# First stage of a two-block transformer kernel: a new written order, and the B matrices turned whole

## The chip, the cores and the metric

The kernel runs on one core of one Trainium2 chip. The metric is the device time of one execution in microseconds (us). A change within about 0.2% of it can't be told from no change.

## The reference, cut to what matters

Two transformer blocks stand one after the other, on 256 tokens of 1024 features, all float32. Only the beginning of both matters here.

The first block modulates its input: for the latent stream `x` and the context stream `ctx`

```
mod_lat = silu(c) @ ada_w[0] + ada_b[0]
sh1, sc1, ga1, sh2, sc2, ga2 = split(mod_lat, 6)
u_lat = rms_norm(x, g_mix[0]) * (1 + sc1) + sh1
qkv   = u_lat @ na_wqkv
```

and the same with `c_ctx` and `ctx`. So the first large product, `@ na_wqkv`, needs the first two sixths (shift and scale) of `c @ ada_w`, which is 8 MB of weights.

The second block has a state-space mixer (S5) with 64 groups of 64 complex states. Its recurrence is computed in chunks of 8 tokens by operator matrices which depend on the weights `lam`, `log_dt`, `B`, `C`, `d` alone. They are wanted only late in the kernel, but they are built at its very start.

## The kernel before, in words

Every large product is split in three float32r products (high by high, high by low, low by high part); `Weights` (from line 245) loads a weight tile (`raw`), writes its high part `whi` by ScalarE (ACT) and its low part `wlo` by VectorE (DVE), in `split`, whose operations have the lines 109 and 112 of the helpers `act` and `tt`.

The **first stage** is the code from line 942 to `spp.close()`. In it

- small vectors, constants, `x`, `ctx` and the S5 weights are loaded. `s5_load` (line 574) loads B (`a_b_re`, `a_b_im`) in two halves each, with the 32 pairs of groups on 32 partitions, into tiles `bt`, and C into tiles `ci`;
- `S5.__init__` (line 600) turns B: for each of the 16 features `h_` there is a turn of 32x64 numbers for the first group of each pair (`T.transpose`, line 620) and, for the second group, a product with the 32x32 identity that writes the lower 64 rows of the result (`T.matmul`, line 618). DVE then makes `bb` and the powers `pw`;
- `x` and `ctx` are turned by TensorE (PE, line 982) and copied to `h` and `hc` by ACT;
- `ada_steps(0, 0)` and `ada_steps(0, 1)` (line 347) are 16 steps, 8 for shift and 8 for scale. A step loads 512 KB of `ada_w` and multiplies; even steps load into a pool of three tiles `ada`, odd steps into two tiles `stl` that later hold the normed input. The eighth step of each row of steps ends in `adacc` (DVE), two turns (PE, line 367) and `mods` (DVE); the last also gives `scg`. `ada(n)` is the next n steps;
- `rstd` (line 442) squares `h` and `hc` on ACT, sums on PE (line 428), takes the reciprocal on DVE (line 432) and spreads it by PE (line 439); `prep_vectors` (line 211) turns the small vectors (line 214) into `vt`;
- `s5.c()` (line 703) turns C and makes `dd`; `s5.e(r)` (line 733) makes the matrices `e` of operator group r on DVE: 8 products into `tm` and 4 sums into `e`, all 128x512. `operators(r)` (line 968) is `k1` (PE, from `e` and `cbk`), `et` (four turns of `e` on PE, four copies on ACT, four stores to `edr`) and `k2`. There are four groups, r = 0 to 3;
- `normed` (line 461) makes the normed, modulated input `x` in high and low parts: for each of 8 feature tiles and both streams `t` (DVE), `xh` (ACT), `xl` (DVE).

The second stage then begins with the product for the first head pair (`lead`, 96 matmuls of 128x256) and for the first group of values (another 96), lines 302 to 304; its other tiles lie in pools opened after the tiles `e`, `kt` and their like are given back (`spp.close()`).

**What sets the order.** Each engine runs its instructions in one compiled order. Inside `tc.manual_schedule(...)` (line 974) the engines named, and that is all of them, take the instructions in the order in which they are written. Behind the block a scheduler orders the instructions by its own model, before the run; it may also put such later instructions between those of the block. A DMA is issued by the queue of the engine on which it is written: SP (`dma`), ACT (`dma_a`) or POOL (`G.dma_start`). The four `raw` loads of `w_first` are written on SP between steps 10 and 11 of the modulation.

Of the kernel before, what the change touches and what calls it, by code (L numbers as in the profile page):

```python
# [8 lines left out]
F32 = mybir.dt.float32  # L9
# [73 lines left out]
def _build(ctx, tc, I, out, dbg):  # L83
    nc = tc.nc
    V, A, G, T = nc.vector, nc.scalar, nc.gpsimd, nc.tensor
    MUL, ADD, SUB = ALU.mult, ALU.add, ALU.subtract
    dma, dma_a = nc.sync.dma_start, nc.scalar.dma_start
# [26 lines left out]
    def stt(o, a, s, b, op0, op1):  # L114
        V.scalar_tensor_tensor(out=o, in0=a, scalar=s, in1=b, op0=op0, op1=op1)  # L115

    def ts(o, a, s1, op0, s2=None, op1=None, e=None):
        e = e or V
        if s2 is None:
            e.tensor_scalar(out=o, in0=a, scalar1=s1, scalar2=None, op0=op0)  # L120
        else:
            e.tensor_scalar(out=o, in0=a, scalar1=s1, scalar2=s2, op0=op0, op1=op1)
# [18 lines left out]
    cst = const.tile([128, _NC], F32, name="cst")  # L141
# [25 lines left out]
    gsw = [swg[:, 0:64], swg[:, 64:128]]  # L167
# [221 lines left out]
    def modcol(l, n, kt, v):  # L389
        return mods[l][:, n * 8 + kt, v:v + 1]  # L390
# [92 lines left out]
    def new_x(pool, tag, n):  # L483
        return [[pool.tile([128, n], F32R, tag=f"{tag}{p}{k}", name=f"{tag}{p}{k}") for k in range(KT)]
                for p in "hl"]
# [88 lines left out]
    def s5_load(pp):  # L574
        lt = spare(4, "lt")[0:32].rearrange("p (i n) -> p i n", i=4)
        ld = pp.tile([32, 2], F32, name="ld")
        dr = pp.tile([32, 32], F32, name="dr")
        bt = [[pp.tile([128, 1024], F32, tag=f"e{1 + r}{j}", name=f"bt{r}{j}")[0:32] for j in range(2)]
              for r in range(2)]
        ci = [pp.tile([128, 1024], F32, tag=f"e3{i}", name=f"ci{i}").rearrange("p (b d n) -> p b d n", b=8, d=2)  # L580
              for i in range(2)]
        todo = [(lt[:, 0, :], I["a_lam_re_2"][0].rearrange("(g j) p -> g (j p)", j=2)),
                (lt[:, 1, :], I["a_lam_im_2"][0].rearrange("(g j) p -> g (j p)", j=2)),
                (ld, I["a_log_dt_2"][0].rearrange("(g j) -> g j", j=2))]
        for r, nm in ((0, "a_b_re_2"), (1, "a_b_im_2")):
            for j in range(2):
                todo.append((bt[r][j], I[nm][0].rearrange("(g j) p h -> g j (p h)", j=2)[:, j]))
        for r, nm in ((0, "a_c_re_2"), (1, "a_c_im_2")):
            for d in range(2):
                todo.append((ci[r][:, :, d, :], I[nm][0].rearrange("(b g) h p -> (g h) b p", g=8)))  # L590
        todo.append((dr, I["a_d_2"][0].rearrange("(a b) -> a b", b=32)))
        return (lt, ld, dr, bt, ci), [
            lambda o=o, i=i, n=n: (G.dma_start if 7 <= n < 11 else dma_a)(out=o, in_=i) for n, (o, i) in enumerate(todo)]

    class S5:


        def __init__(self, pp, loads):
# [11 lines left out]
                T.transpose(pl[:, i * 32:(i + 1) * 32], lt[:, i, :], ident[0:32, 0:32])  # L610
            pb = [bank("s") for _ in range(2)]
            for r in range(2):
                for j in range(2):
                    b_ = bt[r][j].rearrange("g (p h) -> g h p", h=16)
                    for h_ in range(16):
                        o_ = pb[r][64 * j:64 * j + 64, 32 * h_:32 * h_ + 32]
                        if j:
                            T.matmul(o_, lhsT=b_[:, h_, :], rhs=ident[0:32, 0:32])
                        else:
                            T.transpose(o_, b_[:, h_, :], ident[0:32, 0:32])  # L620
            bt = [x_.rearrange("p (h g) -> p g h", h=16) for x_ in pb]
            L = pp.tile([128, 128], F32, name="L")
            cp(L, pl[:, 0:128])
# [64 lines left out]
        def tables(self):  # L688
            pp, pw, pf, ph, u = self.pp, self.pw, self.pf_, self.ph_, self.u
            self.pw2 = [pp.tile([128, 32, 8], F32, name=f"pz{i}") for i in range(2)]  # L690
            for i in range(2):
                for r in range(4):
                    ts(self.pw2[i][:, 8 * r:8 * r + 8, :].rearrange("p (q j) t -> p q j t", q=4),
                       pw[i][:, 0:8, :].rearrange("p t (q r j) -> p r q j t", q=4, r=4)[:, r], 1.0, MUL, 0.0, ADD, e=G)
            for i in range(3):
                cmul((ph[:, 0], ph[:, 1]) if i == 2 else u[(i + 1) % 2], u[i % 2], u[i % 2], self.t_)

            self.em = [[pp.tile([128, 1024], F32, tag=f"e{r}{i}", name=f"e{r}{i}").rearrange(
                "p (q j t h) -> p q j t h", q=4, j=2, t=8) for i in range(2)] for r in range(3)]
            self.tm = [spare(2 + i, f"tm{i}").rearrange("p (n t h) -> p n t h", n=4, t=8) for i in range(2)]  # L700
            self.kt = [None] * 4

        def c(self):
            pp, ct, ci, dr = self.pp, self.ct, self.ci, self.dr

            for r in range(2):
                for i in range(2):
                    pc = bank("s")
                    for b in range(4):
                        T.transpose(pc[:, b * 128:(b + 1) * 128], ci[r][:, 4 * i + b].rearrange("p d n -> p (d n)"), ident)  # L710
                    for j in range(2):
                        pj = slice(64 * j, 64 * j + 64)
                        act(ct[r][pj, 16 * i:16 * i + 16, :],
                            pc[pj].rearrange("p (g j h) -> p g j h", j=2, h=16)[:, :, j, :], AF.Copy)
            for r in range(2):
                act(self.pf_[:, r], self.pw[r][:, 1:9, :], AF.Copy)
            self.dd = dd = pp.tile([32, 32, 32], F32, name="dd")
            pdk = bank("s")
            T.transpose(pdk[0:32, 0:32], dr, ident[0:32, 0:32])
            act(dr, pdk[0:32, 0:32], AF.Copy)  # L720
            tt(dd, dr.unsqueeze(2).to_broadcast([32, 32, 32]), ident[0:32, 0:32].unsqueeze(1).to_broadcast([32, 32, 32]),
               MUL)
            self.kst = [spare(10 + i, f"kst{i}").rearrange("p (r q j x) -> p r q j x", r=4, q=2, j=2) for i in range(2)]
            self.em.append([pp.tile([128, 1024], F32, tag=f"e3{i}", name=f"e3{i}").rearrange(
                "p (q j t h) -> p q j t h", q=4, j=2, t=8) for i in range(2)])

        def save(self):
            for i in range(2):
# [194 lines left out]
    with ExitStack() as sa:  # L923
# [11 lines left out]
        with ExitStack() as s0:  # L935
# [28 lines left out]
            def ada(n):  # L964
                for _ in range(n):
                    ada_step()

            def operators(r):
                s5.k1(r)
                s5.et(r)  # L970
                s5.k2(r)

            w = I["na_wqkv"][0]
            with tc.manual_schedule(engines={ENG.PE, ENG.DVE, ENG.Activation, ENG.SP, ENG.Pool}):
                for f in vloads[0:2] + [lambda: dma(out=cst, in_=I["cst"])] + sloads[0:7] + xloads + small_loads[0:15]:
                    f()
                prep_cond(cc, sc)
                s5 = S5(pp, loads)
                for k in range(KT):
                    ps = bank("x")  # L980
                    for t in range(4):
                        T.transpose(ps[:, t * 128:(t + 1) * 128], xt[t][k // 4][:, (k % 4) * 128:(k % 4) * 128 + 128],
                                    ident)
                    act(h[k], ps[:, 0:256], AF.Copy)
                    act(hc[k], ps[:, 256:512], AF.Copy)
                for f in sloads[7:]:
                    f()
                s5.tables()
                for f in small_loads[15:-1]:
                    f()  # L990
                ada(4)
                s5.c()
                s5.e(0)
                ada(2)
                act(small, h[KT - 2][:, 0:1], AF.Sqrt, bias=eps, scale=0.0)
                r_ = rstd(512, 0, None, "s")
                prep_vectors(va)
                ada(3)
                s5.e(1)
                operators(0)  # L1000
                ada(2)
                w_first = [Weights(wpairs(w, D, 0), by_k=True)]
                ada(2)
                s5.e(2)
                small_loads[-1]()
                stt(gna, gna, 0.125, swg[:, 208:272], MUL, MUL)
                ts(gsw[0], gsw[0], 0.125, MUL)
                operators(1)
                ada(3)
            w_first.append(Weights(wcols(w, 2 * D, 256), by_k=True))  # L1010
            x = new_x(xa, "x", 512)
            normed(x, r_, 512, lambda k, v: scg[0][:, 0, k, v:v + 1], lambda k, v: modcol(0, 0, k, v))
            operators(2)
            s5.e(3)
            operators(3)
# [881 lines left out]
```

## Time and profile before

| | |
|---|---|
| median of 3 runs | 1781.26 us (1780.39 to 1783.09) |
| the profiled execution's own time | 1785.5 us |
| its span, first to last instruction | 1783.8 us |
| PE busy | 1701.6 us, 95% of the span |
| DVE busy | 1177.1 us, 66% |
| ACT busy | 798.1 us, 45% |
| POOL busy | 446.9 us, 25% |
| granted TensorE clock, mean | 0.981 |

The shares are averages over all stages; the change is in the first 5% of the span, where they are different. "DVE busy" and its like count the instructions alone. Where a row ends in brackets, it says how long the engine stood idle before the instruction, and which instruction ended the wait.

### The profile page before, as it was taken

The numbers are of one execution on the slowest core, as the hardware profiler recorded it, in microseconds if no ns is written. First come the engines' busy times: TensorE is split into PE (matmuls) and PEld (weight loads), VectorE is DVE, ScalarE is ACT, GpSimd is POOL, SyncE is SP. The second block draws the span as 40 slices with busy tenths as digits, with TensorE's granted clock in tenths as the row PEclk, the third lists the DMA queues.
The fourth block names the chain that finished last, engine by engine and source line by source line (L and its number), as shares of the span: only waits on it lengthen the run. The fifth ranks groups of instructions, "written<-read, shape, count | busy, mean of one in ns | idle before, by whom it ended". The sixth has DMA issues, their size and how long they took to land. (4 is left out here: it accounts for less than half of the span.)

```text
span 1783.8 us, 33896 instructions
## 1 busy us (share of the span) xinstructions
PE 1701.6 (95%) x13257; PEld 1506.2 (84%) x13257; DVE 1177.1 (66%) x2412; ACT 798.1 (45%) x1463; POOL 446.9 (25%) x619
## 2 busy tenths in 40 slices
PE   6899999999999999999998999989999999999999
PEld 5687888876777777888877999969899999789998
DVE  6877777855545343447975756767577788858674
ACT  5544444434323131324674545536444465444443
POOL 4022112136897000040002000231331322434130
PEclk9899999999999999999998999999999999999999
DMA  9566445333766554332206766788458474345853
GB/s 281 179 157 185 131 149 159 97 119 128 245 202 205 179 159 141 94 95 71 72 25 166 206 194 182 237 274 224 130 154 234 141 225 135 103 114 162 234 148 89
DMA packets 428288, 286.57 MB, mean 161 GB/s; under 512 B 37513, under 2 KB 405336, under 8 KB 428128
## 3 DMA queue, kind: packets, MB, share of 16 engines
q1 hardware_dynamic: 422064, 271.53, 52.4%
q0 software_dynamic: 2800, 7.29, 1.3%
q10 hardware_dynamic: 3264, 5.59, 0.9%
q8 instruction: 104, 1.70, 0.4%
q14 instruction: 56, 0.46, 0.1%
HBM read 271.41 MB, written 17.15 MB: 162 GB/s over the span
## 5 line engine op out<-in xcount | busy, mean ns | idle before, releaser
L109 ACT ACTIVATE whi<-raw 128x1024 fp32r<-128x1024 f32 (+2 forms) x388 | 389.8, 1012 | 476.7 <-PE g L295 360.7
L112 DVE TENSOR_TENSOR wlo<-raw,whi 128x1024 fp32r<-128x1024 f32 (+2 forms) x388 | 463.1, 1198 | 187.3 <-ACT whi L109 182.9
L296 PE MATMUL g<-xh,wlo 128*128 128x256 f32 (+1 forms) x1216 | 375.6, 309 | 5.5 <-DVE wlo L112 5.2
L294 PE MATMUL g<-xh,whi 128*128 128x256 f32 (+1 forms) x1216 | 375.3, 310 | 1.3 <-ACT xh L109 1.2
L295 PE MATMUL g<-xl,whi 128*128 128x256 f32 (+1 forms) x1216 | 374.6, 308 | 0.0
L294 PE MATMUL g<-oh,whi 128*128 128x256 f32 (+1 forms) x1056 | 331.6, 315 | 3.5 <-ACT oh L109 1.4
L296 PE MATMUL g<-oh,wlo 128*128 128x256 f32 (+1 forms) x1056 | 331.3, 314 | 0.0
L295 PE MATMUL g<-ol,whi 128*128 128x256 f32 (+1 forms) x1056 | 330.9, 313 | 0.0
L296 PEld LDWEIGHTS g<-xh,wlo 128*128 128x128 f32 x1216 | 235.3, 194 | 18.2 <-DVE wlo L112 7.7
L294 PEld LDWEIGHTS g<-xh,whi 128*128 128x128 f32 x1216 | 235.0, 194 | 16.4 <-ACT whi L109 3.5
L295 PEld LDWEIGHTS g<-xl,whi 128*128 128x128 f32 x1216 | 235.5, 194 | 9.7
L294 PEld LDWEIGHTS g<-oh,whi 128*128 128x128 f32 x1056 | 198.0, 188 | 24.0 <-issue 3.7
L295 PEld LDWEIGHTS g<-ol,whi 128*128 128x128 f32 x1056 | 198.3, 188 | 15.3 <-issue 1.1
L296 PEld LDWEIGHTS g<-oh,wlo 128*128 128x128 f32 x1056 | 198.3, 188 | 14.3 <-issue 0.2
L302 PE MATMUL g<-whi,xh 128*128 128x256 f32 x560 | 166.3, 297 | 3.8 <-ACT whi L109 1.6
L303 PE MATMUL g<-wlo,xh 128*128 128x256 f32 x560 | 161.0, 288 | 0.1
L304 PE MATMUL g<-whi,xl 128*128 128x256 f32 x560 | 160.0, 288 | 0.1
L115 DVE SCALAR_TENSOR_TENSOR h<-g,mods,h 128x256 f32<-128x256 f32 x64 | 30.9, 483 | 141.7 <-PE g L296 141.7
L302 PEld LDWEIGHTS g<-whi,xh 128*128 128x128 f32 x560 | 108.2, 193 | 12.8 <-issue 8.9
L303 PEld LDWEIGHTS g<-wlo,xh 128*128 128x128 f32 x560 | 108.5, 194 | 0.8 <-issue 0.3
L304 PEld LDWEIGHTS g<-whi,xl 128*128 128x128 f32 x560 | 107.4, 193 | 1.2 <-issue 0.8
L109 ACT ACTIVATE oh<-t 128x256 fp32r<-128x256 f32 (+1 forms) x108 | 51.3, 482 | 126.4 <-DVE t L112 126.4
(329 smaller groups left out, 2840.5 us busy)
## 6 DMA issues: line engine op xcount, KB each, us to landing
raw<-mlp_w SPq DMA_DIRECT2D x128, 512.0 KB, 4.3
ada<-ada_w SPq DMA_DIRECT2D x88, 512.0 KB, 5.1
raw<-ffn_w_up SPq DMA_DIRECT2D x88, 512.0 KB, 5.0
raw<-ffn_w_down SPq DMA_DIRECT2D x32, 384.0 KB, 3.8
raw<-ffn_w_down SPq DMA_DIRECT2D x32, 320.0 KB, 3.3
raw<-na_wqkv SPq DMA_DIRECT2D x32, 256.0 KB, 4.8
raw<-a_w_glu SPq DMA_DIRECT2D x16, 512.0 KB, 7.1
raw<-w_kv SPq DMA_DIRECT2D x16, 512.0 KB, 3.6
```

The lines of the kernel that those rows point to most:

```text
L109: last[0] = A.activation(out=o, in_=i, func=f, **kw)
L112: (e or V).tensor_tensor(out=o, in0=a, in1=b, op=op)
L115: V.scalar_tensor_tensor(out=o, in0=a, scalar=s, in1=b, op0=op0, op1=op1)
L294: T.matmul(ps, lhsT=a, rhs=xh[k][:, s0:s1], start=first, stop=False)
L295: T.matmul(ps, lhsT=a, rhs=xl[k][:, s0:s1], start=False, stop=False)
L296: T.matmul(ps, lhsT=b, rhs=xh[k][:, s0:s1], start=False, stop=last_)
L302: T.matmul(ps, lhsT=xh[k][:, t0:t0 + 128], rhs=a, start=first, stop=False)
L303: T.matmul(ps, lhsT=xh[k][:, t0:t0 + 128], rhs=b, start=False, stop=False)
L304: T.matmul(ps, lhsT=xl[k][:, t0:t0 + 128], rhs=a, start=False, stop=last_)
```

## The change

1. B is loaded with one DMA for each of its two parts, 32 rows of 8 KB, in place of two of 4 KB rows, into one tile of 2048 columns. It is turned by 16 turns of 32x128 numbers for each part; the products with the identity are gone. The two tiles `e{r}0`, `e{r}1` of a group become halves of one tile `e{r}`, made by `em_tile`. The first slice of the small S5 loads is thereby 5 long, not 7; C is loaded by the same DMAs as before.
2. The written order of the first stage is another: `rstd` and `prep_vectors` come ahead of `e(0)` and `c()`; the modulation steps come as 4, 8, 4 and not as 4, 2, 3, 2, 2, 3; group 1 comes behind the block; `normed` comes into it. Groups 2 and 3 stood behind it before as well.

The turns of C, in `c()`, are as they were.

```
-        bt = [[pp.tile([128, 1024], F32, tag=f"e{1 + r}{j}", name=f"bt{r}{j}")[0:32] for j in range(2)]
-              for r in range(2)]
+        bt = [pp.tile([128, 2048], F32, tag=f"e{1 + r}", name=f"bt{r}")[0:32] for r in range(2)]
...
-            for j in range(2):
-                todo.append((bt[r][j], I[nm][0].rearrange("(g j) p h -> g j (p h)", j=2)[:, j]))
+            todo.append((bt[r], I[nm][0].rearrange("(g j) p h -> g (j p h)", j=2)))
...
-            lambda o=o, i=i, n=n: (G.dma_start if 7 <= n < 11 else dma_a)(out=o, in_=i) for n, (o, i) in enumerate(todo)]
+            lambda o=o, i=i, n=n: (G.dma_start if 5 <= n < 9 else dma_a)(out=o, in_=i) for n, (o, i) in enumerate(todo)]
...
-                for j in range(2):
-                    b_ = bt[r][j].rearrange("g (p h) -> g h p", h=16)
-                    for h_ in range(16):
-                        o_ = pb[r][64 * j:64 * j + 64, 32 * h_:32 * h_ + 32]
-                        if j:
-                            T.matmul(o_, lhsT=b_[:, h_, :], rhs=ident[0:32, 0:32])
-                        else:
-                            T.transpose(o_, b_[:, h_, :], ident[0:32, 0:32])
+                b_ = bt[r].rearrange("g (n h) -> g h n", h=16)
+                for h_ in range(16):
+                    T.transpose(pb[r][:, 32 * h_:32 * h_ + 32], b_[:, h_, :], ident[0:32, 0:32])
...
+        def em_tile(self):
+            r = len(self.em)
+            t = self.pp.tile([128, 2048], F32, tag=f"e{r}", name=f"e{r}").rearrange(
+                "p (i q j t h) -> p i q j t h", i=2, q=4, j=2, t=8)
+            self.em.append([t[:, i] for i in range(2)])
...
                 ada(4)
-                s5.c()
-                s5.e(0)
-                ada(2)
                 act(small, h[KT - 2][:, 0:1], AF.Sqrt, bias=eps, scale=0.0)
                 r_ = rstd(512, 0, None, "s")
                 prep_vectors(va)
-                ada(3)
+                s5.e(0)
+                s5.c()
+                ada(8)
+                operators(0)
                 s5.e(1)
-                operators(0)
-                ada(2)
                 w_first = [Weights(wpairs(w, D, 0), by_k=True)]
-                ada(2)
-                s5.e(2)
-                small_loads[-1]()
-                stt(gna, gna, 0.125, swg[:, 208:272], MUL, MUL)
-                ts(gsw[0], gsw[0], 0.125, MUL)
-                operators(1)
-                ada(3)
+                ada(4)
+                x = new_x(xa, "x", 512)
+                normed(x, r_, 512, lambda k, v: scg[0][:, 0, k, v:v + 1], lambda k, v: modcol(0, 0, k, v))
+            small_loads[-1]()
+            stt(gna, gna, 0.125, swg[:, 208:272], MUL, MUL)
+            ts(gsw[0], gsw[0], 0.125, MUL)
             w_first.append(Weights(wcols(w, 2 * D, 256), by_k=True))
-            x = new_x(xa, "x", 512)
-            normed(x, r_, 512, lambda k, v: scg[0][:, 0, k, v:v + 1], lambda k, v: modcol(0, 0, k, v))
+            operators(1)
+            s5.e(2)
             operators(2)
             s5.e(3)
             operators(3)
```

## Rows read from the trace of the kernel before

**Rows 1.** Stretches: length; busy us (instructions) of PE, PEld, DVE, ACT, POOL; clock; DMA share; GB/s.
```profile
31.14:49.44 18.30, 10.73 (x105) 6.20 (x101) 11.30 (x20) 9.98 (x30) 2.09 (x4) 0.71 0.90 251
49.44:76.59 27.15, 21.95 (x264) 13.51 (x256) 24.55 (x44) 16.39 (x36) 0.00 (x0) 0.82 0.71 243
76.59:97.03 20.44, 20.44 (x173) 19.70 (x174) 19.17 (x39) 11.52 (x26) 0.19 (x1) 1.00 0.28 90
```

**Rows 2.** In order of time, 90 to 106: start, duration, engine, line, operation.
```profile
90.30 1.21 ACT L109 ACTIVATE t<-g 128x256 f32<-128x256 f32 x4 [1.56 <-PE g L304]
...
96.34 0.69 DVE L112 TENSOR_TENSOR e<-tm,tm 128x512 f32<-128x512 f32 x1
99.34 0.44 PE L774 MATMUL s<-cst,kt 128*128 128x128 f32 x2
99.87 0.42 DVE L512 TENSOR_REDUCE ss<-t 128x4 f32<-128x256 f32 x1 [2.83 <-ACT et L109]
...
105.39 0.64 PE L360 MATMUL x<-ada,sl 128*32 128x256 f32 x8 [1.19 <-ACT sp L109]
```

**Rows 3.** What SP's queue waited for, 90 to 112: us in total, times, longest.
```profile
SPq L355 <- PE s L774: 2.0, 1, 2.0
```

**Rows 4.** PE in order of time, 10 to 20: half of the turns of B.
```profile
10.57 1.09 PE L620 MATMUL s<-cst,bt 32*64 32x32 f32 x16
11.59 3.73 PE L618 MATMUL s<-cst,bt 32*64 32x32 f32 x32
```

**Rows 5.** In order of time, 19 to 27: turns of x, DVE behind B, last copy.
```profile
19.96 6.17 PE L982 MATMUL x<-cst,sth 128*128 128x128 f32 x32
20.07 0.69 DVE L112 TENSOR_TENSOR t<-s,sm 128x512 f32<-128x512 f32 x1 [1.84 <-PE s L618]
...
26.63 0.43 ACT L109 ACTIVATE hc<-x 128x256 f32<-128x256 f32 x1
```

**Rows 6.** DMA issued from 9.5 to 10.5: KB, us to landing.
```profile
sth<-ctx SPq DMA_DIRECT2D x1, 256.0 KB, 5.5
```

**Rows 7.** In order of time, 33 to 59.
```profile
33.12 1.28 ACT L109 ACT_TABLE_LOAD   x1
33.14 1.21 DVE L112 TENSOR_TENSOR dd<-dr,cst 32x1024 f32<-32x1024 f32 x1 [2.00 <-ACT dr L109]
34.28 1.27 DVE L112 TENSOR_TENSOR tm<-pz,bb 128x512 f32<-128x512 f32 x2
...
40.13 0.37 ACT L109 ACTIVATE sd<-x,cst 128x128 f32<-128x128 f32 x1 [0.51 <-PE x L428]
...
42.37 0.94 DVE L432 RECIPROCAL sd<-sd 128x128 f32<-128x128 f32 x1
...
46.18 0.56 DVE L125 COPY vt<-x 128x384 f32<-128x384 f32 x1 [2.87 <-PE x L214]
...
49.28 0.24 DVE L112 TENSOR_TENSOR mods<-x,vt 128x8 f32<-128x8 f32 x2 [0.78 <-PE x L367]
...
58.71 2.36 DVE L112 TENSOR_TENSOR wlo<-raw,whi 128x1024 fp32r<-128x1024 f32 x2 [1.10 <-DMA edr<-et]
```

**Rows 8.** In order of time, 66 to 77.
```profile
66.30 1.22 DVE L112 TENSOR_TENSOR wlo<-raw,whi 128x1024 fp32r<-128x1024 f32 x1
...
71.34 0.42 DVE L125 COPY adacc<-x 128x256 f32<-128x256 f32 x1
...
76.59 0.39 PE L302 MATMUL g<-whi,xh 128*128 128x256 f32 x1
```

**Rows 9.** DVE's groups by form, 76.59 to 97.03: busy, mean ns, idle before.
```profile
L115 DVE SCALAR_TENSOR_TENSOR xl<-t,mods,xh 128x256 fp32r<-128x256 f32 x16 | 6.9, 482 | 1.8 <-ACT xh L109 1.8
```

**Rows 10.** PE's groups by form, 76.59 to 105.39: busy, mean ns, idle before.
```profile
L766 PE MATMUL s<-cst,e 128*128 128x128 f32 x16 | 2.7, 279 | 0.0
```

**Rows 11.** DMAs issued by SP from 51 to 52: KB each, us to landing.
```profile
stl<-ada_w SPq DMA_DIRECT2D x2, 256.0 KB, 4.7
```

**Rows 12.** ACT's groups by form, 49.4 to 100.8: busy, mean ns, idle before.
```profile
L109 ACT ACTIVATE xh<-t,mods 128x256 fp32r<-128x256 f32 x16 | 7.1, 500 | 2.8 <-DVE t L115 2.8
```

More of the change, by code (lines that the diff above doesn't have):

```diff
@@ L577, in s5_load @@
         dr = pp.tile([32, 32], F32, name="dr")
-        bt = [[pp.tile([128, 1024], F32, tag=f"e{1 + r}{j}", name=f"bt{r}{j}")[0:32] for j in range(2)]
-              for r in range(2)]
-        ci = [pp.tile([128, 1024], F32, tag=f"e3{i}", name=f"ci{i}").rearrange("p (b d n) -> p b d n", b=8, d=2)
-              for i in range(2)]
+        bt = [pp.tile([128, 2048], F32, tag=f"e{1 + r}", name=f"bt{r}")[0:32] for r in range(2)]
+        ci = pp.tile([128, 2048], F32, tag="e3", name="ci").rearrange("p (i b d n) -> p i b d n", i=2, b=8, d=2)
+        ci = [ci[:, i] for i in range(2)]
         todo = [(lt[:, 0, :], I["a_lam_re_2"][0].rearrange("(g j) p -> g (j p)", j=2)),
@@ L696, in tables @@
                 cmul((ph[:, 0], ph[:, 1]) if i == 2 else u[(i + 1) % 2], u[i % 2], u[i % 2], self.t_)
-            self.em = [[pp.tile([128, 1024], F32, tag=f"e{r}{i}", name=f"e{r}{i}").rearrange(
-                "p (q j t h) -> p q j t h", q=4, j=2, t=8) for i in range(2)] for r in range(3)]
+            self.em = []
+            self.em_tile()
+            self.em_tile()
+            self.em_tile()
             self.tm = [spare(2 + i, f"tm{i}").rearrange("p (n t h) -> p n t h", n=4, t=8) for i in range(2)]
@@ L723, in c @@
             self.kst = [spare(10 + i, f"kst{i}").rearrange("p (r q j x) -> p r q j x", r=4, q=2, j=2) for i in range(2)]
-            self.em.append([pp.tile([128, 1024], F32, tag=f"e3{i}", name=f"e3{i}").rearrange(
-                "p (q j t h) -> p q j t h", q=4, j=2, t=8) for i in range(2)])
+            self.em_tile()
+        def em_tile(self):
[3 more added lines that the diff above has]
+            self.em.append([t[:, i] for i in range(2)])
         def save(self):
@@ L974, in _build @@
             with tc.manual_schedule(engines={ENG.PE, ENG.DVE, ENG.Activation, ENG.SP, ENG.Pool}):
-                for f in vloads[0:2] + [lambda: dma(out=cst, in_=I["cst"])] + sloads[0:7] + xloads + small_loads[0:15]:
+                for f in vloads[0:2] + [lambda: dma(out=cst, in_=I["cst"])] + sloads[0:5] + xloads + small_loads[0:15]:
                     f()
@@ L985, in _build @@
                     act(hc[k], ps[:, 256:512], AF.Copy)
-                for f in sloads[7:]:
+                for f in sloads[5:]:
                     f()
```

## The prediction

> **What bounds the kernel now.** The page's table of slices first: over the whole span PE is busy 95%, but its first slice and the stretches up to 76.59 us are looser, and only there does the change act. I then read the busy time by stretch. Before the first large product PE is busy 10.73 of 18.30 and 21.95 of 27.15 us, DVE 11.30 and 24.55; from 76.59 to 97.03 PE is full and DVE busy 19.17 of 20.44 [rows 1]. The bounds are where `e(1)` begins (49.44), the first large product begins (76.59) and the last `e` ends (97.03); so from `e(1)` on DVE has 43.7 us of work in 47.6. The reader is to see that a freer PE gains nothing there by itself.
>
> Next, the order of time around the end of this stage. The second stage's first DVE instruction, `ss`, starts at 99.87, when the last copies of operator group 3 end; its operand, the squares of the lead product, was ready at 91.5, 8 us earlier. SP's first load of that stage waits for line 774 of group 3 [rows 2, 3]. Both write tiles that lie where `e` and `kt` lay, so I read this as one **release**: the second stage's tiles come free with the last operator group. That group follows the last `e` on DVE, which ends at 97.03; `ss` follows 2.84 us later. PE meanwhile lives on the 192 products of the first pair and the first values, and runs out of them just as the norm chain arrives: it waits 1.19 us at 105.39 [rows 2]. So the time of this stage is set by DVE's path to the last `e`, not by the start of the first product.
>
> **The change part by part.** The sum is made on DVE's path, in the order of time.
>
> *Turns of B.* Removed are two blocks of 32 rows on line 618, 3.73 us each [rows 4]. A turn of 32x128 isn't in the trace. From below it costs what a 32x64 turn does: 16 start within 1.02 us, 0.064 each; from above what a 128x128 one does, 32 in 6.17, 0.193 [rows 4, 5]. So 32 turns end between 2.0 and 6.2 us after 10.57, at 12.6 to 16.8, and not at 19.96. I take neither end: the next thing is then the arrival of `ctx`. A `ctx` load issued between 9.5 and 10.5 lands 5.5 us later, at 15 to 16 [rows 6]. I take 16.0 as the start of the turns of x, 4.0 earlier; the last copy then ends at 23.1, not 27.06. The range for the turns costs at most 0.8 us of that. By the Trainium skill (TensorE: Matmul & The Clock Gate, section LDWEIGHTS) the load of the stationary side goes by its columns, not its rows, so that 128 columns take some 107 ns: an estimate of 3.4 us for 32 turns, with no run here that shows it; the sum would be the same.
>
> The two fewer DMAs on ACT's queue carry the same bytes; 0, between -1 and +1 us in the arrival of `ctx`, since these loads share engines with it. On DVE the wait of 1.84 us for the second half of B goes [rows 5]: **-1.84**. What is late next is nothing on DVE until the powers are done.
>
> *`rstd` and `prep_vectors` first.* ACT needs 7.4 us from its table load at 33.12 to the end of `sd` at 40.50 [rows 7]; begun at 23.1, that is 30.5. DVE is through with its powers and phases at 29.3 (now at 31.14, where the wait ahead of `dd` begins, less 1.84) and takes the reciprocal at 30.5. Behind it come the same 2.87 us of wait for PE as in the row, the copy of `vt` at 34.3 and, 0.8 later, `e(0)` for 8.1 us (34.28 to 42.37), to 43.2; `dd` 1.1; `adacc` 0.4 [rows 8], its wait of 0.78, `mods`. So `e(1)` begins at 45.8 and not at 49.44: **-3.6** in all, the 1.84 among them. The two waits that `dd` and the rest had of ACT, 2.00 us, are gone [rows 7]; in their place DVE waits 1.2 us for the squares.
>
> *Modulation steps 4, 8, 4.* Step 4 now stands behind `rstd`, the small turns and `c()` on PE; until it has run, step 10's load has no tile, and on SP everything behind it waits: step 11 and the four `raw` loads. I put that at about 38, some 7 us later than now. Step 11's two loads now go ahead of the `raw` loads. Also, step 8 waits on PE until DVE has copied the first `adacc`, at 44.8, so the loads of steps 14 and 15 go out near 48 and land 4.7 us later [rows 11], near 53. Cover: `e(1)` keeps DVE until 53.9. Cost 0; without the cover up to 3 us of the product's start, of which the release knows nothing.
>
> *Group 1 and `e(2)` behind the block.* The same instructions. The scheduler does put such work between those of the block: at 66.30 a `wlo` of the later `w_first[1]` stands inside the hand-ordered `e(2)` [rows 8]. In DVE's 1.10 us before `w_first`'s `wlo` [rows 7] `e(2)` can now run; between 0 and -1.1, I take **-0.5**. The stores of group 1 on ACT's queue and the bias store on POOL's go with them; POOL is idle throughout [rows 1]; 0.
>
> *`normed` inside the block.* Its DVE work is written t, xl, t, xl, so each of 16 `xl` waits for its `xh`, about 0.5 us [rows 9, 12]. Now it waits 1.8 us in all. The gaps are filled if the scheduler puts the 24 operations of `e(2)` and `e(3)`, some 0.64 each [rows 7], into them: **0**, between 0 and +7.8 (below). The merged `e` tiles change no reader; 0.
>
> From `e(1)` to the last `e` nothing else differs. The sum is -3.6 - 0.5 = **-4.1 us**: last `e` at 92.9, release near 95.8, the rest shifted. The profiled execution's own time is 1785.5 us, 1.7 over its span and 4.2 over the median of the runs shown; 1785.5 - 4.1 = 1781.4 there is **1777.2 us** for the median. The first product starts far earlier: `w_first`'s `wlo` ended 11.6 us after `e(1)` began, so at 57.4, and 0.4 + 5.3 later [rows 7, 8] the product, at 63, 13.5 us before. Most of that isn't time won, for groups 1 and 2 then have to be done beside it.
>
> **The rivals.** *PE's end decides, not the release.* If `e(2)` and `e(3)` fill all of DVE's gaps and the later weights' `wlo` fall behind them, the start counts. From 76.59 to its wait PE had 27.6 us: 192 products at 20.44/173 = 0.118 us [rows 1] are 22.7, so one group (its 16 turns are in the stretch [rows 10]) costs 4.9. Group 1 fits into PE's waits ahead of the product, group 2 doesn't: -13.5 + 4.9 = -8.6, 1772.7 us. Against it: `ss` waited although its operand lay ready.
>
> *The gain is eaten.* Earlier weights bring a further pair of `wlo`, 2.4 us [rows 7], ahead of the last `e`, or group 1 is put where the hand had put it: -4.1 + 2.4 = -1.7, 1779.6 us. Here belongs that the title's words don't fit: the output matrices C are turned as before, it is B that changes, so nothing comes from C.
>
> *Slower: DVE's written order in `normed`.* Unfilled, each t, xh, xl takes 0.48 + 0.50 + 0.48 = 1.46 us [rows 9, 12], 23.4 for 16, where the 32 DVE operations alone take 13.8 (6.9/16 each); less the 1.8 us of waits now, +7.8. An `xh` that comes behind another copy adds to it, as ACT is already busy 11.52 of 20.44 us [rows 1]; I take 0.1 us for each, 1.6: -4.1 + 9.4 = +5.3, 1786.6 us. It decides from 7.7 us of such waits on. For it: the order is fixed within the block. Against it: there is work to put in between. The Trainium skill (TensorE: Matmul & The Clock Gate, the table at its head) has VectorE take its queue strictly in order; by that, nothing at run time could fill a gap that the compiled order leaves. The trace agrees in that DVE stood idle 2.83 us at 99.87 [rows 2].
>
> **How the numbers follow.** A measurement tells from no change what is over 0.2%, 3.56 us. Forecast 0.45, of which 0.29 is beyond that bound; PE's end 0.16; eaten 0.22; slower 0.17. Faster 0.29 + 0.16 = 0.45; same 0.16 + 0.22 = 0.38; slower 0.17. The range goes from 1770, PE's end less 2.7 for group 2 half hidden, to 1786, where most of the slower rival begins to be left out.
>
> **What would show it.** In the profile after: B turned by about 14 to 17, last `hc` copy near 23, reciprocal near 30.5, `e(1)` near 46, first product at 60 to 66, last `e` near 93, `ss` near 96. The forecast is wrong if `ss` no longer follows group 3, if DVE has more than 4 us of waits on `xh`, or if the stretches behind 110 us differ in length by more than the shift.

## The result, and the profile after

The changed kernel takes 1790.94 us in the median (1788.90 to 1793.15); the kernel before took 1782.01 beside it. The ratio is 1.0057, with an interval of 1.0037 to 1.0076: **slower by 8.9 us between the medians and by about 10 by the ratio**, where 4.1 us less had been forecast. Measured twice more, in e5 and e15 below, it is 1.0034 (1.0018 to 1.0051) and 1.0067 (1.0055 to 1.0080). The profiled execution took 1793.15 us, with a span of 1791.4, 7.6 over the span before; its mean granted clock is the same 0.981.

First the busy times by stretch of the kernel after, with the columns of [rows 1]; the first three rows answer to the three there.

```profile
31.14:49.44 18.30, 10.63 (x112) 6.20 (x110) 13.25 (x24) 7.29 (x23) 0.55 (x1) 0.87 0.76 252
49.44:76.59 27.15, 20.47 (x242) 14.03 (x234) 23.32 (x40) 14.89 (x31) 0.00 (x0) 0.76 0.71 240
76.59:97.03 20.44, 19.72 (x201) 17.22 (x189) 15.69 (x31) 11.98 (x28) 0.18 (x1) 1.00 0.46 146
112.00:150.00 38.00, 30.76 (x247) 24.47 (x247) 27.31 (x83) 17.22 (x44) 10.02 (x14) 0.91 0.36 107
150.00:1791.40 1641.40, 1586.42 (x12167) 1413.12 (x12166) 1068.66 (x2113) 726.60 (x1285) 417.03 (x558) 0.99 0.54 157
```

And two stretches of the kernel before which do not stand among its rows above:

```profile
112.00:150.00 38.00, 34.61 (x291) 28.07 (x289) 25.85 (x82) 15.21 (x40) 9.32 (x13) 0.96 0.62 177
150.00:1783.80 1633.80, 1578.79 (x12100) 1407.33 (x12098) 1067.62 (x2110) 724.57 (x1281) 414.65 (x558) 0.99 0.54 157
```

The last row of each says where the loss is. At 150 us PE of the changed kernel has 12167 instructions left, before it had 12100. These are 67 more, and 1586.42 - 1578.79 = 7.63 us of busy time, as much as the span has grown. So everything is lost ahead of 150 us, as **work that PE has not done by then**. In the last 38 us before that mark PE is busy 30.76 us, where it was 34.61, and does 247 instructions, where it did 291. So 44 of the 67 are lost between 112 and 150 us, and 23 ahead of 112.

Next DVE in order of time, from the reciprocal on; among these rows stands PE's first large product.

```profile
33.60 0.95 DVE L432 RECIPROCAL sd<-sd 128x128 f32<-128x128 f32 x1 [4.03 <-ACT sd L109]
...
47.44 1.28 DVE L112 TENSOR_TENSOR tm<-pz,bb 128x512 f32<-128x512 f32 x2
...
64.34 0.47 DVE L115 SCALAR_TENSOR_TENSOR t<-h,scg,s 128x256 f32<-128x256 f32 x1
...
66.22 1.23 DVE L112 TENSOR_TENSOR wlo<-raw,whi 128x1024 fp32r<-128x1024 f32 x1 [0.21 <-ACT whi L109]
66.64 0.58 PE L302 MATMUL g<-whi,xh 128*128 128x256 f32 x1 [3.17 <-ACT xh L109]
67.37 0.48 DVE L115 SCALAR_TENSOR_TENSOR xl<-t,mods,xh 128x256 fp32r<-128x256 f32 x1
67.76 0.47 DVE L115 SCALAR_TENSOR_TENSOR t<-hc,scg,s 128x256 f32<-128x256 f32 x1
70.03 1.23 DVE L112 TENSOR_TENSOR wlo<-raw,whi 128x1024 fp32r<-128x1024 f32 x1 [1.80 <-ACT whi L109]
71.43 0.48 DVE L115 SCALAR_TENSOR_TENSOR xl<-t,mods,xh 128x256 fp32r<-128x256 f32 x1 [0.17 <-ACT xh L109]
...
87.99 0.69 DVE L112 TENSOR_TENSOR e<-tm,tm 128x512 f32<-128x512 f32 x1
...
98.79 0.48 DVE L115 SCALAR_TENSOR_TENSOR xl<-t,mods,xh 128x256 fp32r<-128x256 f32 x1 [0.58 <-ACT xh L109]
99.19 0.47 DVE L115 SCALAR_TENSOR_TENSOR t<-hc,scg,s 128x256 f32<-128x256 f32 x1
100.24 0.49 DVE L115 SCALAR_TENSOR_TENSOR xl<-t,mods,xh 128x256 fp32r<-128x256 f32 x1 [0.58 <-ACT xh L109]
100.65 0.74 DVE L512 TENSOR_REDUCE ss<-t 128x4 f32<-128x256 f32 x2
```

The reader is to see four things. `e(1)` begins at 47.44, 2.0 us sooner than before, and the first product at 66.64, 10 us sooner than [rows 8]. The last `e` ends at 88.68, 8.3 us sooner than [rows 2]. But the last `xl`, which before was written by 89.6 us, ends at 100.7. And `ss` no longer follows group 3: it follows that last `xl`, as the squares it sums wait for products of it. From 94 us on DVE has nothing but pairs of t and `xl`, 1.45 us each, with 0.58 us of idle time in each: there is no `e` left to fill them.

The groups of DVE from 49.4 to 105 us (columns as in [rows 9]) count these waits, which were 1.8 us in [rows 9]:

```profile
L115 DVE SCALAR_TENSOR_TENSOR xl<-t,mods,xh 128x256 fp32r<-128x256 f32 x16 | 7.7, 483 | 7.3 <-ACT xh L109 7.3
L112 DVE TENSOR_TENSOR wlo<-raw,whi 128x1024 fp32r<-128x1024 f32 x6 | 7.3, 1223 | 2.3 <-ACT whi L109 2.3
```

Last, what PE waited for from 60 to 150 us (us in total, times, longest), the two largest; in the kernel before the same view begins with 2.7 us for `p` and has no wait for `xh`.

```profile
PE sc L1139 <- ACT p L109: 6.3, 3, 5.5
PE g L302 <- ACT xh L109: 5.6, 3, 3.2
```

`p` is the first softmax of the attention. PE at the end of its first wait for it, in the kernel before and after:

```profile
130.32 0.39 PE L1142 MATMUL sc<-a,q 128*128 128x256 f32 x1 [1.90 <-ACT p L109]
```

```profile
131.80 0.58 PE L1139 MATMUL sc<-a,q 128*128 128x256 f32 x1 [5.54 <-ACT p L109]
```

The softmax itself comes only 1.5 us later (its first instruction on ACT starts at 130.97, before at 129.49). But before PE still had products of the second group of values to make, up to 127.4. Their weights are loaded by these instructions of SP's queue, in the kernel before and after:

```profile
91.39 3.38 SPq L268 DMA_DIRECT2D raw<-na_wqkv  x2
```

```profile
134.36 1.15 SPq L268 DMA_DIRECT2D raw<-na_wqkv  x2
```

After the change they are issued 43 us later, behind the first `p`.

### The profile page after: what moved, and what is told of

It reads as the page before. It is cut to its first block, busy times and chain, and to the rows that moved or that the text cites. A ratio compares the mean times of both kernels' runs of the same rounds, so it can differ in the third digit from the quotient of the medians.

```text
span 1791.4 us, 33756 instructions
## 1 busy us (share of the span) xinstructions
PE 1699.3 (95%) x13193; PEld 1500.3 (84%) x13193; DVE 1176.6 (66%) x2412; ACT 799.4 (45%) x1463; POOL 447.9 (25%) x619
## 5 line engine op out<-in xcount | busy, mean ns | idle before, releaser
L295 PEld LDWEIGHTS g<-ol,whi 128*128 128x128 f32 x1056 | 198.3, 188 | 15.3 <-issue 1.1
```

What stands on the lines that cost most here:

```text
L295: T.matmul(ps, lhsT=a, rhs=xl[k][:, s0:s1], start=False, stop=False)
```

## The experiments

All are timed beside the kernel before on the same chip; a ratio is to that. Ratio and medians are worked out apart and can differ by up to 0.1%. The theories named in the expectations: **A**, the written order t, xl, t, xl inside the block; **B**, the rest of the new order; **C**, the new B and the merged tiles; **D**, a chance order of the scheduler later on. M, M2, P and X came up on the way.

**e1. `normed` behind the block again.**

```
-                x = new_x(xa, "x", 512)
-                normed(x, r_, 512, ...)
...
             w_first.append(Weights(wcols(w, 2 * D, 256), by_k=True))
+            x = new_x(xa, "x", 512)
+            normed(x, r_, 512, ...)
```

> The changed kernel with one thing undone: `new_x` and `normed` stand behind the hand-ordered block again, behind the second weights, as they did before. Theory A (the written order t, xl, t, xl in the block delays x and costs the time): nearly all of the 9 us goes, 1777 to 1782 us; DVE's 7.3 us of waits on `xh` fall under 3, the last xl comes near 90 and not at 100.2, ss follows at once. Rival B (the other reordering costs: rstd ahead of e(0), steps 4, 8, 4, group 1 behind the block): 1788 to 1792 us, and x is late for another reason. Rival D (a chance order of the scheduler further on, behind 110 us): no telling, but the product's end at 102.2 stays.

1784.51 us, 1.0022 (1.0008 to 1.0035). The waits on `xh` are 1.5 us, the last `xl` ends at 81.2, `ss` starts at 98.12. Of a loss of 0.34 to 0.67%, 0.22% is left.

**e2. `normed` in the block, with a lag.** The 16 pairs are written so that `xl` of pair n stands behind t of pair n + 2.

```
+                lag, todo_ = 2, []
...
+                        todo_.append((x[1][k][:, s], t[:, s], modcol(0, 0, k, v), x[0][k][:, s].bitcast(F32)))
+                        if len(todo_) > lag:
+                            o, a_, m_, b_ = todo_.pop(0)
+                            stt(o, a_, m_, b_, ADD, SUB)
```

> The changed kernel with normed left in the block, but each xl written two places later, so that two other t stand between an xh and its xl. What is computed, and where the block ends, is the same. Theory A: as in e1, 1777 to 1782 us, waits on xh under 3 us. If only the place in the block counts (the scheduler can't mix other work in), not the order of t and xl: 1788 to 1792. Rival B: 1788 to 1792.

1779.89 us, 1.0005 (0.9990 to 1.0019): the loss is gone, by moving 16 instructions by two places. DVE's `xl` from 49.4 to 105 us, its first `wlo` of the second values, and PE's wait for the first `p` in e2:

```profile
L115 DVE SCALAR_TENSOR_TENSOR xl<-t,mods,xh 128x256 fp32r<-128x256 f32 x16 | 7.6, 481 | 1.3 <-ACT xh L109 1.3
```

```profile
103.74 1.22 DVE L112 TENSOR_TENSOR wlo<-raw,whi 128x1024 fp32r<-128x1024 f32 x1
...
129.11 0.39 PE L1151 MATMUL sc<-a,q 128*128 128x256 f32 x1 [1.90 <-ACT p L109]
```

Everything else of the change is in this kernel, so B and C by themselves are not the cause. But neither is there a gain, though its last `e` ends at 93.8, near the 92.9 of the forecast.

**e3. The kernel before, with `normed` moved into the block** (the two lines of e1 the other way, behind its `ada(3)`).

> The kernel before with one part of the change alone: new_x and normed moved into the block, at its end. Theory A: slower by 5 to 10 us, 1787 to 1792; waits on xh rise from 1.8 to 6 us or more. Rival B: within 3 us of before, 1779 to 1785.

1784.68 us, 1.0025 (1.0011 to 1.0038), waits on `xh` 6.5 us, last `xl` at 99.5. The part of the change that A names costs 4.4 us alone, less than the whole loss. The weights of the second values go out late here too, at 125.73, and their `wlo` run from 139.83 on. Yet PE waits no more than 0.5 us for a `p` up to 150 us, since the first softmax comes 7 us sooner than before, not later:

```profile
122.50 0.69 ACT L109 ACTIVATE p<-sc,st 128x512 f32<-128x512 f32 x1 [2.23 <-DVE st L850]
```

So an x as late as this doesn't have to bring the long wait at `p`.

**e4. The kernel before, with the new B alone** (the first point of the change).

> The kernel before with the other part alone: B loaded whole and turned in 32 turns of 32x128, and the e tiles merged. Theory A: 1.84 us less on DVE ahead of the powers, 1779 to 1782 us, no loss. Rival C (the merged tiles or the changed loads cost): over 1785.

1781.82 us, 1.0010 (0.9998 to 1.0021). No loss, and the 1.84 us of DVE's wait brought nothing that shows.

**e5. The changed kernel again**, on the chip of e6 to e8.

> The changed kernel as it is, beside the kernels below on one chip. That the loss belongs to the kernel: 9 us slower than before, ratio 1.004 to 1.008, and so 9 us over e2, which differs from it by the place of 16 instructions. If it was a matter of the chip: under 1.003.

1787.67 us, 1.0034 (1.0018 to 1.0051).

**e6. The second weights behind `e(2)`.**

```
-            w_first.append(Weights(wcols(w, 2 * D, 256), by_k=True))
             operators(1)
             s5.e(2)
+            w_first.append(Weights(wcols(w, 2 * D, 256), by_k=True))
             operators(2)
```

> The changed kernel, the second weights (loads, whi, wlo) written behind group 1 and e(2), and not ahead of group 1; normed stays as it is in the block. Theory A alone (t, xl, t, xl costs all of the 9 us): the time stays at 1788 to 1792. Theory A with a second part (normed in the kernel before cost 4.4 us only, in e3; the other half comes from the second weights' wlo, which now stand among the first xl and wait 2.3 us for whi and its loads): 1784 to 1787 us, and the first three xl of the stream come 3 us sooner.

1784.30 us, 1.0018 (1.0004 to 1.0032): 3.4 us under e5, though the two intervals overlap. The last `xl` ends at 96.5, in e5 at 99.0: the two `wlo` among the first `xl` have a share in the delay of x.

**e7. The kernel before without `e(3)`**: the test of the prediction's release. Group 3 is made from the matrices of group 0, so a part of the computation is left out.

```
-            s5.e(3)
+            s5.em[3] = s5.em[0]
             operators(3)
```

> The kernel before with group 3 made from the matrices of group 0: e(3), 8.1 us of DVE, is left out, and with it part of the computation; PE, ACT and the DMAs do what they did. The prediction's release (DVE's path to the last e sets the stage): 8 us less, 1771 to 1774 us. Rival (PE's work not yet done at 150 us counts, and ss could wait without harm): 1777 to 1782 us.

1788.53 us, 1.0037 (1.0024 to 1.0049): with 8.1 us of DVE work less the kernel is **slower**, by 7.6 us between the medians. PE at the first `p` of e7:

```profile
130.78 0.58 PE L1142 MATMUL sc<-a,q 128*128 128x256 f32 x1 [8.04 <-ACT p L109]
```

Its x isn't late, and there is no `normed` in a block; yet the wait at the first `p` is there, even longer, and the `wlo` of the second values come at 146 us, not at 105. So the compiled order behind the stage changed, and that alone is worth some 7 us.

**e8. The changed kernel with the old B.**

> The changed kernel with the old B: halves, 64 turns and products, separate e tiles; the new order alone. Theory A: the order alone carries the loss, and B's 3.6 us shift of PE at the beginning is lost behind other waits: 1788 to 1792 us. Rival (an earlier first part is worth something): 2 to 4 us above e5.

1792.83 us, 1.0065 (1.0048 to 1.0083). The order alone carries the loss. It lies 5.2 us over e5, the changed kernel on the same chip, but by the ratio level with e15; whether the new B takes something off is not shown.

**e9. The kernel before, the second values written into the next turn** (theory M).

```
+                if pr == 1:
+                    fill[-1:-1] = v_steps(1, 0) + v_steps(1, 1)
-                if pr // 2 < 3:
+                elif pr // 2 < 3 and pr:
```

> The kernel before; the first stage untouched. In the second stage the first half of the products of the second group of values (48 matmuls, 5.8 us of PE) is written into the turn of the second head pair and so behind the first softmax; nothing is left out. Theory M (the changed kernel loses where PE waits 5.5 us for the first p at 131.8, as these products stand behind that p and not ahead of it): PE waits 6 to 8 us for the first p, and the time is 4 to 7 us over before, 1785 to 1788. Rival (that wait is made up later, and the loss comes from the delay of x alone): within 2 us of before, 1779 to 1783.

1781.79 us, 1.0014 (1.0000 to 1.0028). The wait is 3.1 us and not 6: the scheduler put other products there. It took the cover away only in part and did not decide.

**e10. e2 without `e(3)`** (the edit of e7; the same part of the computation is left out).

> e2 with group 3 made from the matrices of group 0, so that e(3), 8.1 us of DVE, is left out, and with it part of the computation. Unlike in e7, the compiled order of DVE behind the stage stays that of e2. The prediction's release (DVE's path to the last e sets the time): 5 to 8 us under e2, 1772 to 1775. Theory P (PE's supply of products sets it, and only the 2.4 us that PE waits at 103.6 in e2 can be won): 0 to 3 us under e2, 1777 to 1780.

1780.10 us, 0.9996 (0.9982 to 1.0010). Here the order behind the stage stayed. DVE's last `e` and first `ss`:

```profile
83.77 0.69 DVE L112 TENSOR_TENSOR e<-tm,tm 128x512 f32<-128x512 f32 x1
...
94.52 1.07 DVE L512 TENSOR_REDUCE ss<-t 128x4 f32<-128x256 f32 x3 [7.67 <-PE s L774]
```

The last `e` is 9.4 us earlier than in e2 and `ss` 4.2, and the ratios differ by 0.0009. `ss` still waits for group 3, so the release is real, but now for its work on PE, behind other work of PE. The 5 to 8 us that the release would have given are not there: DVE's path to the last `e` does not set the time.

**e11. e2 and e6 together.**

> e2 and e6 together: normed in the block with each xl two places later, and the second weights written behind e(2). If the two delays of x (order of t and xl; wlo among the first xl) add up: 1 to 3 us under e2, 1777 to 1779, and the first stream of xl without a wait over 1 us. If only where the third weights' wlo fall counts, as theory M has it: same as e2, 1779 to 1781.

1782.79 us, 1.0009 (0.9995 to 1.0022). `ss` at 93.41, 6.5 us before [rows 2], and no gain; PE instead waits 3.3 us for a load of `ada_w` and 2.3 for `p`.

**e12. The kernel before with the new B and with `normed` in the block as in e2.**

> The old order with the new B (e4) and with normed in the block, each xl two places later. Against e3 it differs, beside B, in the places of xl alone. Theory A: the 4.4 us of e3 are gone, 1779 to 1782. If it is the place in the block that cost in e3, not the order of t and xl: 1783 to 1786.

1781.03 us, 0.9997 (0.9986 to 1.0008). Against e3 the 4.4 us are gone: it is the order of t and `xl`, not the block. (The new B is in e12 too, but e4 gives it no gain.)

**e13. The changed kernel with the second values' weights loaded ahead of the chains.** 

```
+            q1, v1 = qk_steps(1, False), v_steps(1, 0)
+            q1[0]()
+            v1[0]()
...
+                if pr == 0:
+                    fill += q1[1:-1] + v1[1:] + q1[-1:]
```

> The changed kernel; the first stage and the order of t and xl stay as they are. In the second stage the loads of the second pair's weights and of the second values' weights are written ahead of the attention chains. In the compiled order the two wlo of the second values then stand ahead of the first score, and not 40 us behind it. Theory M2 (x late by 11 us makes the compiled order put the products of the second values behind the first p; the 48 or so matmuls that PE has not done by 150 us are the loss): the wait at the first p falls from 5.5 to under 2.5 us, the products by 150 us rise by 40 or more, and the time falls by 5 to 7 us against e15. Theory X (PE lost its time to the late x before 112 us and the wait at p is no part of the loss): within 2 us of e15.

1790.12 us, 1.0046 (1.0030 to 1.0063): 3.1 us under e15, less than the 5 to 7 expected, and the two intervals overlap. The loads go out at 103.94, the wait at `p` falls to 0.2 us, but the `wlo` stand behind the second pair's norm and run at 128.45, and PE waits there:

```profile
129.72 0.58 PE L303 MATMUL g<-wlo,xh 128*128 128x256 f32 x1 [3.68 <-DVE wlo L112]
```

**e14. The same edit on the kernel before**, the control.

> The same edit on the kernel before, as a control: the second values' wlo stand ahead of the first score there already, so both theories expect no change, 1779 to 1783. If the edit is worth something by itself, e13 has to be read against this run.

1780.91 us, 0.9997 (0.9987 to 1.0007).

**e15. The changed kernel, on the chip of e13.**

> The changed kernel as it is, on the same chip as e13: 1786 to 1792, as in e5.

1793.19 us, 1.0067 (1.0055 to 1.0080).

**e16. e2 with the edit of e13.**

> The same edit on e2 (xl two places later in the block). Theory M2: no change against e2 and e14, within 2 us of before, as the order there was right already. If the earlier x of e2 becomes worth something with the weights loaded ahead: 2 to 4 us under before, 1776 to 1778.

1782.86 us, 1.0013 (1.0005 to 1.0022). Nothing is won by it.

**e17. A lag of one place** (the 2 of e2 is a 1).

> The changed kernel with each xl written one place later, half of what e2 does; everything else as in e15. The last xl comes earlier than the 100 us of the changed kernel, and the compiled order has the two wlo of the second values ahead of the first score, as in e2. Theory M2 (the order behind the stage carries the loss): within 2 us of before, 1779 to 1782. Theory X (each us of delay of x costs about as much): 3 to 5 us over before, 1783 to 1785, if x comes halfway.

1781.38 us, 1.0012 (0.9996 to 1.0027), last `xl` at 86.1, the `wlo` of the second values ahead of the first `p`. The time fits M2 by its range, but lies 2.7 us over the median beside it; the run does not tell M2 from X.

**e18. e13 with the values first** (`fill += v1[1:] + q1[1:]`).

> e13 with the products of the second values written ahead of those of the second pair, so that both the two wlo and the 48 products stand ahead of the first softmax in the compiled order (in e13 the wlo came at 128 us, behind the second pair's norm, and PE waited 3.7 us for them). First stage and x as in the changed kernel. Theory M2: the waits at the first p and on wlo fall under 3 us together, and the time under that of e13, 1783 to 1787. Theory X: as the changed kernel, 1788 to 1793.

1782.37 us, 1.0017 (1.0006 to 1.0028). x is as late as in the changed kernel: waits on `xh` 6.6 us, last `xl` at 99.8. But the `wlo` of the second values come ahead of the first `p`:

```profile
117.00 2.90 DVE L112 TENSOR_TENSOR wlo<-raw,whi 128x1024 fp32r<-128x1024 f32 x2 [1.88 <-ACT whi L109]
```

and PE has no wait at `p` from 60 to 150 us, where it had 6.3 us. Of a loss of 0.34 to 0.67%, 0.17% is left, **with the first stage untouched**. Two things changed at once, however: the first `p` also comes earlier, at 122.33 on ACT and not at 130.97. And this edit was not run on the kernel before; only the one of e13 was (e14: no change).

The runs side by side, with what PE had left at 150 us in the profile, above the 12100 of the kernel before:

| run | ratio | PE instructions left, over before |
|---|---|---|
| changed kernel (first, e5, e15) | 1.0057, 1.0034, 1.0067 | +67, +55, +71 |
| e8, e7 | 1.0065, 1.0037 | +84, +53 |
| e13, e6, e9, e18 | 1.0046, 1.0018, 1.0014, 1.0017 | +48, +42, +23, +12 |
| e2, e10, e11, e12, e14 | 1.0005, 0.9996, 1.0009, 0.9997, 0.9997 | -8, -8, -8, +2, +1 |
| e4, e16, e17 | 1.0010, 1.0013, 1.0012 | -8, -6, 0 |
| e1, e3 | 1.0022, 1.0025 | -2, +2 |

At 7.63/67 = 0.114 us each, the first two rows account for 6 to 10 us, of the 6 to 12 us that these runs lose. No version is faster than the kernel before, clear of the noise.

## Why the prediction was wrong

**The step that failed first is "The release".** The prediction took it that the second stage begins when the tiles `e` and `kt` are given back, and that "the time of this stage is set by DVE's path to the last `e`". It rested on one wait of `ss` [rows 2, 3]. That wait was real, but the time did not follow it: in e10, e2, e11 and e12 the last `e` ends between 84.5 and 97.0 and `ss` starts between 93.4 and 100.2, and the times agree within 0.13%. When `ss` comes sooner, PE waits elsewhere: 2.39 us for `qn` in e2, 2.2 for a load in e10, 3.3 in e11. What the large losses go with is how much of its work PE has done by 150 us, and so how many products stand in the order where the first softmax keeps PE waiting.

**The second is "`normed` inside the block": 0, between 0 and +7.8.** The argument was that 24 operations of `e(2)` and `e(3)` fill the gaps. Nine of them, of `e(2)`, had run before the first t, as the scheduler put them between the instructions of the block. The other 15 did go into the gaps, up to 88.7 us; that used them up, and the last six pairs stood open, with 4.9 of the 7.3 us of waits. And it was part of the harm: from the first t to the last `xl` it is 36.4 us (64.34 to 100.73), before 15.3 (74.27 to 89.6). In e1 and e4 the scheduler wrote several t ahead of the first `xl`, in e2 the lag did; in e3, where the written order stands, it is 27.4 us. The filled gaps are cheap for DVE, but x is wanted by PE, and the prediction had no term for when x is complete. It priced the gaps on a path that did not bind.

**How the late x costs.** PE waits 5.6 us for `xh`, and 23 instructions are missing at 112 us. Then, in the compiled order, the second values, whose load went out at 91.39 before, come behind the first `p`, and 44 more are lost. e18 shows that the order behind the stage carries half of the loss or more: 0.17% stays, of 0.34, 0.57 and 0.67% in the three measurements. At 112 us e18 has 34 instructions more left than the kernel before, at 150 us only 12, so it makes up most of what the late x cost; e3 does the same, from 14 to 2. That moving `xl` alone changes this order is shown by e2 and e17. That it is the lateness of x that does it is only argued: e7 has the long wait with an early x, e3 has a late x without it. Why the scheduler chose as it did stays open.

**The sum to `e(1)`**: -3.6 was forecast, -2.0 came. B was turned at 13.2 (the first row below), within 12.6 to 16.8; the last copy ended at 21.1 and not at 23.1. By the Trainium skill (TensorE: Matmul & The Clock Gate, section LDWEIGHTS) 32 turns had been estimated at 3.4 us; the trace comes near, with 3.74. The reciprocal, forecast for 30.5, came at 33.60. The other three rows of PE and ACT of the kernel after show why:

```profile
9.48 3.74 PE L613 MATMUL s<-cst,bt 32*128 32x32 f32 x32 [2.11 <-DMA bt<-a_b_re]
...
26.71 0.64 PE L360 MATMUL x<-stl,sl 128*32 128x256 f32 x2 [2.75 <-DMA stl<-ada_w]
26.82 0.64 PE L428 MATMUL x<-t,cst 128*32 128x128 f32 x4
...
28.31 0.42 ACT L109 ACTIVATE t<-h 128x256 f32<-128x256 f32 x1 [4.36 <-PE x L428]
```

The sums of the squares (L428) stand on PE behind the fourth modulation step, whose load lands late; the squares wait for their tiles. The prediction gave ACT 7.4 us from the table load to `sd` and left out what stood ahead of the sums on PE: from 21.13 to 33.57 it took 12.4.

**The steps 4, 8, 4, group 1 behind the block, and B** cost nothing that the runs tell from 0: e2 has them all, at 1.0005 (0.9990 to 1.0019). The first product at 66.64 is 3.6 us behind the 63 of the sum, and just outside the forecast 60 to 66.

**The rivals.** "PE's end decides" was nearest in what counts, but its price, 8.6 us less, rested on an earlier start; e11 and e2 have that start and no gain. "DVE's written order in `normed`", the slower one, named the right place, and its 1786.6 us has the right sign. Its price was for DVE's gaps ahead of the last `e`; the gaps came to 7.3 us, which is 5.5 more than before and less than the 7.7 more from which it was to decide, and the last `e` came sooner than forecast. That the time landed on its side is therefore not its mechanism borne out. The strict order of VectorE that the Trainium skill gives (TensorE: Matmul & The Clock Gate, the table at its head) agrees with the 0.58 us in each of the last pairs: nothing from behind them was run in the gap.

All three signs that the prediction named for being wrong are there: `ss` does not follow group 3, the waits on `xh` are over 4 us, and the stretches behind 110 us differ.

**Open.** e1 and e3 lose 0.22 and 0.25% with nothing left over at 150 us; where, was not found, so the count at 150 us is not the whole account. In the kernel before the profiled execution lies 4.2 us over its median, so that differences of one or two us between profiles say little. Why the scheduler's order changed in e7 was not tried.

## What to carry to other kernels

A wait that ends last at the start of a stage is not yet its bound: take work out of the path and see whether the time follows, as e10 did here. Where one engine is busy 95% of the whole, count what it has left at a fixed mark; that number told the large losses, though not the 0.2% of e1 and e3, when five landmarks of the stage had moved forward. In an order written by hand, put a lag of at least one pair between an operation and the one that waits for another engine's answer, and before costing a gap as filled ask what waits for the result that the filling delays.

## What the runs showed of the hardware

A turn of 32 rows by 128 columns takes 3.74/32 = 0.117 us, nearly twice the 0.064 of a 32x64 one [rows 4], and well under the 0.193 of 128x128 [rows 5], whose identity is wider too.

The early start of PE fell at the lower clock. The first product at 66.64 takes 0.58 us, in [rows 8] 0.39. Ahead of it PE had stood still for 3.17 us, and behind it the granted clock is 0.50, the level of 1.2 GHz; in the kernel before PE came to its first product without a wait, at a granted clock of 1.00, the level of 2.4 GHz. In the kernel after and before (columns as in [rows 1]):

```profile
66.64:70.00 3.36, 2.69 (x9) 2.14 (x9) 1.59 (x3) 1.05 (x2) 0.00 (x0) 0.50 0.80 267
```

```profile
76.59:80.00 3.41, 3.41 (x28) 3.08 (x29) 3.41 (x9) 3.10 (x8) 0.00 (x0) 1.00 0.32 123
```
